# A new issue order for a hybrid attention and retention block, found with a longer price for short products

## The chip, the cores and the metric

The kernel runs on one core of one Trainium2 chip. The metric is the device time of one execution in microseconds (us); lower is better. Each time is a median over several executions. "TensorE" (PE in the profile) is the matmul engine, with its weight loads shown apart as PEld; "VectorE" is DVE, "ScalarE" ACT, "GpSimd" POOL; SP is the engine that issues most DMAs.

## The reference, cut to what matters

One decoder block over 512 tokens of 1024 channels, all float32, with one big input projection, two token mixers side by side, and a gated merge:

```python
h = rms_norm(x, norm_pre)
proj = h @ w_in                      # split into q, k, v, gates of both mixers
# mixer A, 8 heads of 64 in 2 groups
kc = compress_blocks(k_cmp_raw, ...) # 31 compressed keys and values per group
s  = einsum('qghd,cgd->qghc', qi, kc) * scale    # the short products of this change
p_c = masked_softmax(s, mask_c); o_c = einsum('qghc,cgd->qghd', p_c, vc)
# ... a selected and a sliding branch, each a masked softmax over up to 512 keys
o_a = g0 * o_c + g1 * o_s + g2 * o_w
# mixer B: retention, 4 heads of 128, chunks of 128 tokens
o_b = normalised(o_inner + o_cross)
y_a = (o_a * silu(z_n)) @ w_nsa_o ; y_b = (o_b * silu(z_r)) @ w_ret_o
merged = sigmoid(m_a) * y_a + sigmoid(m_b) * y_b
x = x + rms_norm(merged @ w_out, norm_post)
```

With 512 tokens there are 8 blocks of 64 keys and up to 16 may be selected, so every causal key is selected, so both long branches of mixer A are causal softmaxes over the same length.

## The kernel before

**Arithmetic.** Every float32 operand is split into a high and a low part (`whi`/`wlo`, `hTh`/`hTl`; ScalarE writes the high part, VectorE subtracts it to get the low part), and one product becomes three matmuls: high by high, high by low, low by high (`mm3`, line 313). Most matmuls have a 128 by 128 stationary operand and 512 moving columns.

**Stages on TensorE, in time.** The first projection `A` (keys and values, 512 columns), `C` (280 columns) and `Q`, the hidden layer of the compressed keys and values, then the weight blocks of `PLAN` (line 29): gate `Z`, `MA`, retention gate `ZR`, `QK`, `VR`, a seven-product block `PAIR` (line 1380), `VR` again, `MB`, and the output projections `NO`, `RO`, with two more seven-product blocks (`seven`), and last `out_seven` (line 1900). The seven-product blocks form sums of quarters of weight matrices with DRAM-to-DRAM accumulating DMAs that GpSimd issues (`add_sums`, lines 440 to 452).

**Work woven in between.** Attention runs between the projections' matmuls. For each tile of 128 queries, from the last to the first, `att_cmp` (line 1028) multiplies the queries of all eight heads with the compressed keys `kc`: seven products of 128 moving columns and one of 64, each with its own stationary operand. Retention does the like in `ret` (line 1406): per tile and head a product of 256 columns and one of 128 (lines 1442 and 1443). Transposes on TensorE (`tr`, line 310) go with nearly every step.

**What sets the order.** The order of all instructions of all engines is written out before launch by a planner, the class `Order` (line 63). Each piece of work is a coroutine that issues its instructions and yields the modelled time at which its next input is ready. `run` (line 135) takes the next coroutine by priority (`PRIOS`, or `OWN` for one instance, line 83) among those whose readiness plus a margin (`MARGINS`, or `OWN`) has passed on the planner's TensorE clock `now`. The main stream of projections has priority 9 and no margin, so it fills whatever is left. A margin is thus spare time between the modelled end of a producer and the place of its consumer in the order.

The planner's price of a matmul comes from `cols_ns` (line 300): where the last dimension of the moving operand is 2 (operands stored as two interleaved halves), 0.4167 ns a column and at least 112 ns; otherwise 0.4418 ns a column plus 2 ns. `mm` (line 305) uses it for more than 64 columns and takes 112 ns for 64 or fewer columns on a wide stationary operand. `PAIR` and `out_seven` use a fixed 215.8 ns.

Other constants that the change touches: `SOON`, `PSOON`, `CSOON` say how many weight halves ahead of the one wanted a split gets top priority (`rank`, line 601); `HOLD` is a pause in `tail_a` (line 835); `FIRST`, `HS`, `ASUMS` say at which point how many of the 27 weight sums are issued, and in which order (lines 435, 454, 1212): three after the signed halves of the input are written, then a group after gate `Z`, then some after each of the eight attention tiles, the rest during retention; `MORE` (line 474) says for which loads two additional weight tiles (named `shorts` in the profile) may be used; `EARLY_OUT` (line 1409) names the retention tiles whose values are first copied out of PSUM, scaled, to a spare buffer, so that the PSUM bank is free sooner.

Of the kernel before, what the change touches and what calls it, by code (L numbers as in the profile page):

```python
# [32 lines left out]
LAG, PE_LAG = 55.0, 60.0  # L33
TAIL = {"act": 110.0, "dve": 82.0, "pool": 45.0}
MARGIN = 20.0
MARGINS = {'att_cmp': 150.0, 'att_head': 150.0, 'att_out': 800.0, 'att_sum': 20.0, 'att_unit': 250.0, 'compress': 0.0, 'ga_split': 100.0, 'gates': 1300.0, 'h_sums': 1000.0, 'hidden': 400.0, 'keep': 600.0, 'kept': 1700.0, 'qk_end': 1300.0, 'ret': 50.0, 'ret_state': 50.0, 'rot_table': 250.0, 's_early': 400.0, 's_late': 1000.0, 'seven_end': 20.0, 'split_lo': 50.0, 'splitter': 250.0, 'tail_a': 50.0, 'tail_c': 0.0, 'tail_m': 1000.0, 'tail_o': 1700.0, 'tail_p': 1000.0, 'tail_q': 1000.0, 'tail_qk': 150.0, 'tail_yb': 600.0, 'tail_z': 100.0, 'x_split': 100.0, 'zr_end': 50.0}
SOON = 4
PSOON = 8
CSOON = 4
ISSUE = 8.0  # L40
SLACK = 1300
WAKE = 7
SIGN, SIGN_LAG = 3, 25000.0
HOLD_C = 300
EARLY = 300
HOLD = 1000
OSUMS = (0, 0, 0, 0, 0, 0, 1, 1)
W2_AT = 12
SUM_ON = 'dve'
ASUMS = (2, 2, 1, 1, 1, 1, 0, 0)  # L50
FIRST, BESIDE = 3, 3200.0
HS = (2, 7, 9)
DVE_BIAS = 700
PRIOS = {'att_block': 1, 'att_cmp': 3, 'att_head': 5, 'att_out': 1, 'att_sum': 1, 'att_unit': 0, 'attention': 2, 'compress': 1, 'edges': 0, 'flip': 5, 'ga_split': 5, 'gates': 5, 'h_low': 3, 'h_split': 5, 'h_sums': 2, 'hidden': 1, 'keep': 2, 'kept': 5, 'more_tiles': 5, 'norms': 2, 'qk_end': 1, 'ret': 2, 'ret_state': 0, 'rot_table': 0, 's_early': 1, 's_late': 2, 'seven_end': 1, 'tail_a': 0, 'tail_c': 1, 'tail_m': 2, 'tail_o': 0, 'tail_p': 3, 'tail_q': 0, 'tail_qk': 3, 'tail_ya': 5, 'tail_yb': 2, 'tail_z': 2, 'tail_zr': 0, 'weight_sums': 3, 'x_split': 2, 'zr_end': 5}
OWN = {'att_block.13': (1, None), 'att_block.21': (None, 20.0), 'att_block.33': (None, 600.0), 'att_block.34': (4, 0.0), 'att_block.36': (None, 150.0), 'att_block.37': (2, 0.0), 'att_block.38': (2, None), 'att_cmp.0': (5, None), 'att_cmp.1': (5, None), 'att_cmp.3': (2, 250.0), 'att_head.19': (1, None), 'att_head.44': (1, None), 'att_head.46': (None, 250.0), 'att_head.47': (None, 250.0), 'att_out.0': (None, 1000.0), 'att_sum.5': (None, 2200.0), 'att_sum.6': (0, 150.0), 'att_sum.7': (0, 600.0), 'att_unit.11': (5, 250.0), 'edges.0': (1, 20.0), 'ga_split.0': (1, 20.0), 'h_low.0': (0, 600.0), 'h_low.2': (2, 800.0), 'h_low.3': (1, 800.0), 'h_low.4': (None, 1000.0), 'h_split.0': (0, None), 'kept.0': (4, None), 'more_tiles.0': (None, 150.0), 'norms.0': (0, None), 'qk_end.0': (2, None), 'qk_end.1': (2, 1700.0), 'qk_end.2': (None, 20.0), 'qk_end.3': (2, None), 'ret.7': (5, 0.0), 'ret_state.2': (None, 150.0), 'ret_state.5': (None, 800.0), 'rot_table.2': (None, 0.0), 'rot_table.3': (0, None), 'rot_table.4': (0, 1700.0), 'signed.0': (4, 3000.0), 'signed.1': (0, 800.0), 'signed.2': (1, 250.0), 'signed.3': (None, 1000.0), 'signed.6': (None, 1300.0), 'split_lo.0': (4, 0.0), 'split_lo.1': (2, 1000.0), 'split_lo.100': (None, 0.0), 'split_lo.104': (None, 1300.0), 'split_lo.105': (2, 1300.0), 'split_lo.106': (None, 2200.0), 'split_lo.107': (3, 1300.0), 'split_lo.109': (None, 4500.0), 'split_lo.118': (0, 250.0), 'split_lo.121': (3, 400.0), 'split_lo.122': (4, None), 'split_lo.123': (0, 50.0), 'split_lo.124': (2, 150.0), 'split_lo.125': (None, 800.0), 'split_lo.127': (2, None), 'split_lo.128': (2, 800.0), 'split_lo.129': (None, 800.0), 'split_lo.130': (4, 150.0), 'split_lo.131': (2, None), 'split_lo.134': (None, 1700.0), 'split_lo.149': (None, 20.0), 'split_lo.160': (None, 100.0), 'split_lo.2': (0, 600.0), 'split_lo.203': (None, 400.0), 'split_lo.21': (None, 150.0), 'split_lo.22': (None, 800.0), 'split_lo.3': (None, 0.0), 'split_lo.4': (0, 100.0), 'split_lo.48': (None, 150.0), 'split_lo.52': (None, 50.0), 'split_lo.60': (None, 100.0), 'split_lo.68': (1, None), 'split_lo.69': (4, 20.0), 'split_lo.70': (2, 400.0), 'split_lo.74': (0, 0.0), 'split_lo.75': (None, 20.0), 'split_lo.76': (None, 800.0), 'split_lo.91': (0, None), 'split_lo.99': (None, 250.0), 'splitter.0': (1, 250.0), 'tail_a.3': (0, None), 'tail_c.2': (None, 100.0), 'tail_m.0': (None, 1000.0), 'tail_m.1': (1, None), 'tail_m.5': (0, 2200.0), 'tail_m.6': (5, 1000.0), 'tail_m.7': (2, 20.0), 'tail_q.0': (4, None), 'tail_q.1': (None, 800.0), 'tail_qk.0': (None, 250.0), 'tail_qk.2': (2, 20.0), 'tail_qk.3': (1, 150.0), 'tail_qk.4': (None, 2200.0), 'tail_qk.5': (3, 1000.0), 'tail_ya.0': (3, None), 'weight_sums.0': (2, 1700.0), 'x_split.0': (1, None), 'zr_end.0': (None, 150.0), 'zr_end.1': (4, 0.0), 'zr_end.3': (0, None)}
HFIRST, HWANT = 0, 0
MORE, MORE2 = range(12, 24), range(24, 28)
EARLY_OUT = ((0, 3), (1, 0), (1, 3))
SKEW = {'MA0': 4, 'Q': 4}
ROPES = ('dve', 'dve', 'dve')  # L60

# [1 line left out]
class Order:  # L63
# [16 lines left out]
    def spawn(self, gen, prio):  # L80
        k = gen.__name__
        i = self.seen[k] = self.seen.get(k, -1) + 1
        own = OWN.get(f"{k}.{i}", (None, None))
        first = PRIOS.get(k, prio) if own[0] is None else own[0]
        margin = MARGINS.get(k, MARGIN) if own[1] is None else own[1]
        self.cos.append([first, self.n, 0.0, gen, margin])
# [96 lines left out]
def block_kernel(ctx: ExitStack, tc, x, xT, x0s, ws, small, w2s, norm_post, rope_r, dmask, out):  # L183
# [47 lines left out]
    def size(a):  # L231
        n = 1
        for k in a.shape[1:]:
            n *= k
        return n
# [62 lines left out]
        return a.rearrange("p (a b) -> p a b", a=2)  # L298

    def cols_ns(b):  # L300
        return max(0.4167 * size(b) + 2.5, 112.0) if b.shape[-1] == 2 else 0.4418 * size(b) + 2

    def mm(ps, a, b, start, stop, r=0.0, cost=None):
        T.matmul(ps, a, b, start=start, stop=stop)  # L304
        return od.pe(cost or (cols_ns(b) if size(b) > 64 else 112 if a.shape[-1] > 64 else 54), r)
# [128 lines left out]
    seq = [(o, a, i >= 4) for s in (psums, sums, osums) for i, (o, a) in enumerate(s)]  # L434
    for i, h in zip(HS, hsums):
        seq[i:i] = [(*h, True)]
# [3 lines left out]
    def add_sums(n):  # L440

        for _ in range(n):
            o, a, add = seq[issued[0]]
            r = [landed.get(v.tensor.name, 0.0) for v in (o, a)]
            r = max(od.busy[v][1] + 1200 if isinstance(v, int) else v for v in r)
            if add:
                G.dma_start(o, a, accum_op=OP.add)
            else:
                G.dma_start(o, a)
            ns = (3200.0 if not add else 4600.0 if a.tensor.name.startswith("in_") else 5600.0) * size(o) / 2048  # L450
            landed[o.tensor.name] = od.sums(od.op("pool", 650.0, r), ns)
            issued[0] += 1

    def weight_sums():
# [7 lines left out]
        od.op("pool", 70.0, zready[0])  # L462
        add_sums(27 - FIRST - sum(OSUMS) - sum(ASUMS))
        od.flags.add("wsum")
# [136 lines left out]
    def rank(p):  # L601

        return lambda: 0 if p <= wanted[0] + (PSOON if p in pairp else CSOON if KD <= p < 2 * KD else SOON) else 4

# [195 lines left out]
    def keysT(kd, off, br, t, r):  # L800
        ps = yield from PT.get()
        yield r + PE_LAG
        for g in range(2):
            e = tr(ps[:, g * P:(g + 1) * P], kd[:, off + g * P:off + (g + 1) * P], ident, r)
        yield e, "act"
        v = ps[:, 0:256].rearrange("p (g c a) -> p g a c", g=2, a=2)
        sl = (slice(None), br, slice(None), slice(None), slice(t * 64, (t + 1) * 64))
        e = act(kA[sl], v, r=e)
        yield e, "dve"
        e = sub_split(kB[sl], v, kA[sl], e)  # L810
        PT.put(ps, e)
        return e
# [8 lines left out]
    def tail_a(t, ps, e, ring):  # L821
# [12 lines left out]
        NAT.put(kn, ev)  # L834
        yield e + HOLD
        yield from keysT(kd, 512, 0, t, e)
# [350 lines left out]
    def att_sum(t, g, po):  # L1187
# [16 lines left out]
        if all(n in od.flags for n in ATT):  # L1204
# [4 lines left out]
            for _ in range(2):  # L1209
                b = yield from PO.get()  # L1210
                PS.put(b)
        n = ASUMS[2 * (NT - 1 - t) + g]
        if n:
# [192 lines left out]
    def ret(hp, t, ps, e):  # L1406
        yield od.need(*[f"att{i}{g}" for i in (2, 3) for g in range(2)])
        vh, vl = yield from VR[hp].get()
        if (hp, t) in EARLY_OUT:
            vf = yield from NAT.get()  # L1410
# [761 lines left out]
```

## Time and profile before

| quantity | value |
|---|---|
| median of three runs | 480.07 us (478.75 to 480.45) |
| the profiled execution | 478.08 us |
| its span, first to last instruction | 476.3 us |
| TensorE busy | 468.8 us, 98% |
| VectorE busy | 411.1 us, 86% |
| ScalarE busy | 337.5 us, 71% |
| GpSimd busy | 43.9 us, 9% |
| mean granted TensorE clock | 0.997 |

The profiled execution took 1.8 us more than its span. Busy time of TensorE is a union of overlapping records: a matmul of 512 columns is recorded with 379 ns, while the next one starts 0.21 to 0.22 us after it. What a matmul costs the engine is therefore read from start to start.

### The profile page before, as it was taken

The page shows a single profiled execution, that of the slowest core. Times are in us where ns is not written, and L with a number is a line of the kernel's source. Part 1 is how long each engine was busy: PE and PEld are TensorE (multiplying, and loading weights), DVE is VectorE, ACT ScalarE, POOL GpSimd, SP SyncE. Part 2 cuts the span into 40 slices and gives each one's busy share as a digit, 9 for nine tenths or more (in the row PEclk, how much of TensorE's full clock was granted, in tenths as well). Part 3 has the DMA queues.
Part 4 walks back from the last instruction along what each step waited for, and adds up shares of the span by engine and source line. Part 5 has one row for each costly group of instructions (what it writes and reads, how often), then busy time and mean ns, then how long its engine had stood idle before and what let it go on. Part 6 is the DMA issues. An engine that isn't in the chain of part 4 may idle for free.

```text
span 476.3 us, 7891 instructions
## 1 busy us (share of the span) xinstructions
PE 468.8 (98%) x2686; PEld 420.1 (88%) x2686; DVE 411.1 (86%) x934; ACT 337.5 (71%) x724; POOL 43.9 (9%) x74
## 2 busy tenths in 40 slices
PE   9999999999999999999999999999999999999994
PEld 8899889988889888888989888998889999988884
DVE  6987899999798898898899998987687867989966
ACT  7976779887879899596698667755345536528853
POOL 3032004003020200101000000012000000000002
PEclk9999999999999999999999999999999999999998
DMA  8866865999997797544677671235974736605828
GB/s 304 330 232 200 261 237 178 290 280 286 322 307 152 143 325 240 111 140 129 135 259 251 203 221 56 67 111 98 326 284 138 230 119 205 202 37 178 253 102 176
DMA packets 30424, 96.65 MB, mean 203 GB/s; under 512 B 3088, under 2 KB 7056, under 8 KB 29584
## 3 DMA queue, kind: packets, MB, share of 16 engines
q1 hardware_dynamic: 23136, 66.66, 41.2%
q0 software_dynamic: 6960, 29.36, 25.8%
q8 instruction: 21, 0.34, 0.3%
q14 instruction: 19, 0.16, 0.1%
q10 hardware_dynamic: 288, 0.14, 0.1%
HBM read 91.42 MB, written 33.03 MB: 261 GB/s over the span
## 4 chain that ended last, share of the span: by engine, by line
PE 97%; DVE 1%; ACT 0%; issue 0%; DVEq 0%
PE bank L304 77%; PE bank L1380 8%; PE bank L1900 8%; PE bank L310 5%; PE bank L2040 1%; ACT whi L256 0%; DVE wlo L268 0%; DVE words L268 0%; DVE words L281 0%; ACT arena_r L256 0%; PE bank L2042 0%; DVE arena_r L268 0%; DVEq L2168 0%; DVE arena_r L264 0%; ACT rsrow L256 0%
## 5 line engine op out<-in xcount | busy, mean ns | idle before, releaser
L256 ACT ACTIVATE whi<-raw 128x512 fp32r<-128x512 f32 x176 | 106.8, 626 | 51.8 <-PE bank L304 34.4
L268 DVE TENSOR_TENSOR wlo<-raw,whi 128x512 fp32r<-128x512 f32 x182 | 119.2, 687 | 6.7 <-ACT whi L256 6.6
L304 PE MATMUL bank<-whi,hTh 128*128 128x512 f32 x192 | 72.1, 396 | 0.2 <-DVE words L268 0.2
L304 PE MATMUL bank<-whi,hTl 128*128 128x512 f32 x192 | 68.9, 379 | 0.0
L304 PE MATMUL bank<-wlo,hTh 128*128 128x512 f32 x192 | 68.8, 379 | 0.0
L304 PE MATMUL bank<-arena_r 128*128 128x256 f32 (+2 forms) x328 | 65.8, 323 | 0.2 <-DVE arena_r L268 0.2
L304 PE MATMUL bank<-arena_r,whi 128*128 128x512 f32 (+1 forms) x208 | 61.5, 371 | 0.0
L256 ACT ACTIVATE words<-words,stat 128x512 f32<-128x512 f32 (+3 forms) x107 | 55.9, 551 | 3.3 <-DVE stat L268 2.8
L256 ACT ACTIVATE arena_r<-bank 128x512 fp32r<-128x512 f32 (+3 forms) x87 | 45.6, 534 | 15.2 <-PE bank L310 14.8
L304 PEld LDWEIGHTS bank<-arena_r 128*128 128x128 f32 x328 | 50.3, 190 | 4.4 <-DVE arena_r L268 0.6
L268 DVE TENSOR_TENSOR arena_r<-bank,arena_r 128x512 fp32r<-128x512 f32 (+2 forms) x72 | 46.7, 656 | 8.7 <-ACT arena_r L256 8.2
L304 PEld LDWEIGHTS bank<-arena_r,whi 128*128 128x128 f32 x208 | 39.1, 189 | 5.0
L304 PE MATMUL bank<-hTh,whi 128*128 128x512 f32 (+1 forms) x120 | 41.5, 346 | 0.0
L304 PEld LDWEIGHTS bank<-whi,hTl 128*128 128x128 f32 x192 | 36.2, 189 | 5.1
L304 PEld LDWEIGHTS bank<-whi,hTh 128*128 128x128 f32 x192 | 36.5, 191 | 4.6 <-DVE words L268 0.8
L304 PE MATMUL bank<-hTl,whi 128*128 128x512 f32 (+1 forms) x120 | 40.5, 337 | 0.0
L304 PE MATMUL bank<-hTh,wlo 128*128 128x512 f32 (+1 forms) x120 | 40.5, 337 | 0.0
L304 PEld LDWEIGHTS bank<-wlo,hTh 128*128 128x128 f32 x192 | 36.4, 189 | 3.8
L268 DVE TENSOR_TENSOR words<-bank,words 128x512 f32<-128x512 f32 (+3 forms) x56 | 34.2, 616 | 6.0 <-ACT words L256 1.9
L268 DVE TENSOR_TENSOR words<-words,words 128x256 f32<-128x256 f32 (+5 forms) x73 | 35.9, 504 | 2.1 <-ACT rsrow L256 0.4
L310 PEld LDWEIGHTS bank<-identr,shorts 128*128 128x128 f32 x276 | 30.7, 140 | 6.6 <-DVE kc L281 0.3
L304 PE MATMUL bank<-arena_r,wlo 128*128 128x512 f32 x96 | 36.4, 379 | 0.0
(201 smaller groups left out, 926.7 us busy)
## 6 DMA issues: line engine op xcount, KB each, us to landing
raw<-in_stream_dram SPq DMA_DIRECT2D x73, 512.0 KB, 4.6
pair<-in_stream_dram POOLq DMA_DIRECT2D x6, 1024.0 KB, 9.5
t<-in_stream_dram POOLq DMA_DIRECT2D x6, 1024.0 KB, 17.7
out<-in_stream_dram POOLq DMA_DIRECT2D x6, 1024.0 KB, 11.3
raw<-s SPq DMA_DIRECT2D x8, 512.0 KB, 4.4
raw<-pair SPq DMA_DIRECT2D x8, 512.0 KB, 4.6
raw<-t SPq DMA_DIRECT2D x8, 512.0 KB, 4.5
raw<-out SPq DMA_DIRECT2D x8, 512.0 KB, 3.8
```

What stands on the lines that cost most here:

```text
L256: S.activation(o, i, func, **kw)
L268: (V if e == "dve" else G).tensor_tensor(o, a, b, op=op)
L304: T.matmul(ps, a, b, start=start, stop=stop)
L310: T.transpose(ps, a, idn)
L1380: T.matmul(ps[m], a, apart(b), start=n in first and s + j == 0, stop=n in last and s + j == 5, skip_group_check=True)
L1900: T.matmul(ps[m], a, apart(b), start=n in first and s + i == 0, stop=n in last and s + i == 5, skip_group_check=True)
L2040: T.matmul(banks[0][:, 0:P], rsrow[:, 0:P], rsrow[:, 0:P], start=True, stop=True)
```

## The change

One line of the planner's price list changes: a product whose moving operand isn't stored in interleaved halves now costs at least 106 ns. With 0.4418 ns a column plus 2, this touches products of 65 to 235 columns: the seven products of 128 columns per query tile with the compressed keys (28 in all), and the retention products of 128 columns (line 1443, 16 in all). Each was priced 58.5 ns and is now priced 106 ns. Then the constants that steer the order were chosen anew. No product is added, removed or changed in size. Of the constants, `MORE`, `EARLY_OUT`, `HS` and `ASUMS` change a little more than a place in the order: which buffer a weight half goes to, one copy out of PSUM, and where the weight sums are issued. The diff, with the long tables cut to the entries spoken of here:

```diff
-MARGINS = {
...
-'att_cmp': 150.0,
-'att_out': 800.0,
-'qk_end': 1300.0,
-'ret': 50.0,
-'splitter': 250.0,
-'tail_p': 1000.0,
-'tail_qk': 150.0,
...
+MARGINS = {
...
+'att_cmp': 400.0,
+'att_out': 150.0,
+'qk_end': 50.0,
+'ret': 20.0,
+'splitter': 1300.0,
+'tail_p': 150.0,
+'tail_qk': 400.0,
...
-SOON = 4
-PSOON = 8
-CSOON = 4
+SOON = 2
+PSOON = 5
+CSOON = 6
...
-HOLD = 1000
+HOLD = 800
...
-ASUMS = (2, 2, 1, 1, 1, 1, 0, 0)
+ASUMS = (6, 0, 2, 2, 2, 2, 0, 0)
 FIRST, BESIDE = 3, 3200.0
-HS = (2, 7, 9)
+HS = (0, 1, 2)
...
-PRIOS = {
...
-'h_split': 5,
-'norms': 2,
-'ret': 2,
...
+PRIOS = {
...
+'h_split': 0,
+'norms': 1,
+'ret': 5,
...
-MORE, MORE2 = range(12, 24), range(24, 28)
-EARLY_OUT = ((0, 3), (1, 0), (1, 3))
+MORE, MORE2 = range(12, 20), range(24, 28)
+EARLY_OUT = ((0, 3), (1, 3))
...
     def cols_ns(b):
-        return max(0.4167 * size(b) + 2.5, 112.0) if b.shape[-1] == 2 else 0.4418 * size(b) + 2
+        return max(0.4167 * size(b) + 2.5, 112.0) if b.shape[-1] == 2 else max(0.4418 * size(b) + 2, 106.0)
```

Of the 32 margins 23 change, of the 41 priorities 24, and of the table `OWN` of single instances 65 entries are changed, added or dropped.

More of the change, by code (lines that the diff above doesn't have):

```diff
@@ L35 @@
 MARGIN = 20.0
-MARGINS = {'att_cmp': 150.0, 'att_head': 150.0, 'att_out': 800.0, 'att_sum': 20.0, 'att_unit': 250.0, 'compress': 0.0, 'ga_split': 100.0, 'gates': 1300.0, 'h_sums': 1000.0, 'hidden': 400.0, 'keep': 600.0, 'kept': 1700.0, 'qk_end': 1300.0, 'ret': 50.0, 'ret_state': 50.0, 'rot_table': 250.0, 's_early': 400.0, 's_late': 1000.0, 'seven_end': 20.0, 'split_lo': 50.0, 'splitter': 250.0, 'tail_a': 50.0, 'tail_c': 0.0, 'tail_m': 1000.0, 'tail_o': 1700.0, 'tail_p': 1000.0, 'tail_q': 1000.0, 'tail_qk': 150.0, 'tail_yb': 600.0, 'tail_z': 100.0, 'x_split': 100.0, 'zr_end': 50.0}
-SOON = 4
-PSOON = 8
-CSOON = 4
+MARGINS = {'att_cmp': 400.0, 'att_head': 150.0, 'att_out': 150.0, 'att_sum': 0.0, 'att_unit': 250.0, 'compress': 20.0, 'ga_split': 20.0, 'gates': 1700.0, 'h_sums': 1300.0, 'hidden': 400.0, 'keep': 1300.0, 'kept': 1300.0, 'qk_end': 50.0, 'ret': 20.0, 'ret_state': 150.0, 'rot_table': 250.0, 's_early': 250.0, 's_late': 1300.0, 'seven_end': 600.0, 'split_lo': 50.0, 'splitter': 1300.0, 'tail_a': 50.0, 'tail_c': 0.0, 'tail_m': 1700.0, 'tail_o': 100.0, 'tail_p': 150.0, 'tail_q': 1000.0, 'tail_qk': 400.0, 'tail_yb': 250.0, 'tail_z': 400.0, 'x_split': 100.0, 'zr_end': 150.0}
+SOON = 2
+PSOON = 5
+CSOON = 6
 ISSUE = 8.0
@@ L49 @@
 SUM_ON = 'dve'
-ASUMS = (2, 2, 1, 1, 1, 1, 0, 0)
+ASUMS = (6, 0, 2, 2, 2, 2, 0, 0)
 FIRST, BESIDE = 3, 3200.0
-HS = (2, 7, 9)
+HS = (0, 1, 2)
 DVE_BIAS = 700
-PRIOS = {'att_block': 1, 'att_cmp': 3, 'att_head': 5, 'att_out': 1, 'att_sum': 1, 'att_unit': 0, 'attention': 2, 'compress': 1, 'edges': 0, 'flip': 5, 'ga_split': 5, 'gates': 5, 'h_low': 3, 'h_split': 5, 'h_sums': 2, 'hidden': 1, 'keep': 2, 'kept': 5, 'more_tiles': 5, 'norms': 2, 'qk_end': 1, 'ret': 2, 'ret_state': 0, 'rot_table': 0, 's_early': 1, 's_late': 2, 'seven_end': 1, 'tail_a': 0, 'tail_c': 1, 'tail_m': 2, 'tail_o': 0, 'tail_p': 3, 'tail_q': 0, 'tail_qk': 3, 'tail_ya': 5, 'tail_yb': 2, 'tail_z': 2, 'tail_zr': 0, 'weight_sums': 3, 'x_split': 2, 'zr_end': 5}
@@ new lines @@
+PRIOS = {'att_block': 1, 'att_cmp': 3, 'att_head': 5, 'att_out': 2, 'att_sum': 1, 'att_unit': 3, 'attention': 3, 'compress': 1, 'edges': 3, 'flip': 2, 'ga_split': 5, 'gates': 2, 'h_low': 1, 'h_split': 0, 'h_sums': 2, 'hidden': 0, 'keep': 0, 'kept': 3, 'more_tiles': 2, 'norms': 1, 'qk_end': 3, 'ret': 5, 'ret_state': 1, 'rot_table': 0, 's_early': 2, 's_late': 2, 'seven_end': 3, 'tail_a': 0, 'tail_c': 1, 'tail_m': 5, 'tail_o': 0, 'tail_p': 0, 'tail_q': 3, 'tail_qk': 3, 'tail_ya': 1, 'tail_yb': 5, 'tail_z': 2, 'tail_zr': 0, 'weight_sums': 2, 'x_split': 2, 'zr_end': 5}
@@ new lines @@
+OWN = {'att_block.13': (1, None), 'att_block.21': (None, 20.0), 'att_block.33': (None, 0.0), 'att_block.34': (4, 100.0), 'att_block.36': (None, 1000.0), 'att_block.37': (0, 0.0), 'att_block.38': (1, 400.0), 'att_block.39': (0, 20.0), 'att_cmp.0': (5, None), 'att_cmp.1': (5, None), 'att_cmp.3': (None, 0.0), 'att_head.19': (1, None), 'att_head.44': (1, None), 'att_head.45': (5, 50.0), 'att_head.47': (None, 1000.0), 'att_out.0': (3, 1300.0), 'att_sum.5': (None, 100.0), 'att_sum.6': (1, 2200.0), 'att_unit.11': (5, 600.0), 'edges.0': (4, 1700.0), 'ga_split.0': (1, 20.0), 'h_low.0': (5, 1700.0), 'h_low.1': (None, 20.0), 'h_low.2': (2, 800.0), 'h_low.3': (1, 800.0), 'h_low.4': (None, 1000.0), 'kept.0': (4, None), 'more_tiles.0': (3, 4500.0), 'norms.0': (1, 100.0), 'qk_end.0': (2, None), 'qk_end.1': (2, 1700.0), 'qk_end.2': (None, 20.0), 'qk_end.3': (3, None), 'ret.0': (2, 0.0), 'ret.7': (4, 100.0), 'ret_state.2': (None, 150.0), 'ret_state.5': (None, 800.0), 'rot_table.3': (1, 4500.0), 'rot_table.4': (0, 1700.0), 'signed.0': (0, 3000.0), 'signed.2': (1, 20.0), 'signed.3': (None, 1000.0), 'signed.6': (None, 1300.0), 'signed.7': (3, None), 'split_lo.0': (3, 150.0), 'split_lo.1': (0, None), 'split_lo.100': (None, 0.0), 'split_lo.104': (None, 1300.0), 'split_lo.105': (2, 1300.0), 'split_lo.106': (None, 2200.0), 'split_lo.107': (3, 1300.0), 'split_lo.109': (None, 4500.0), 'split_lo.110': (3, None), 'split_lo.111': (None, 1700.0), 'split_lo.116': (None, 600.0), 'split_lo.118': (0, 250.0), 'split_lo.121': (3, 400.0), 'split_lo.122': (4, None), 'split_lo.123': (0, 50.0), 'split_lo.124': (2, 150.0), 'split_lo.125': (None, 800.0), 'split_lo.126': (None, 1700.0), 'split_lo.127': (2, 1700.0), 'split_lo.128': (2, 1000.0), 'split_lo.129': (None, 20.0), 'split_lo.130': (4, 800.0), 'split_lo.131': (2, 1000.0), 'split_lo.134': (None, 1700.0), 'split_lo.149': (None, 20.0), 'split_lo.160': (None, 100.0), 'split_lo.162': (None, 50.0), 'split_lo.2': (0, 600.0), 'split_lo.203': (None, 400.0), 'split_lo.21': (None, 150.0), 'split_lo.22': (None, 800.0), 'split_lo.3': (None, 800.0), 'split_lo.4': (0, 100.0), 'split_lo.48': (None, 150.0), 'split_lo.52': (None, 50.0), 'split_lo.59': (None, 150.0), 'split_lo.60': (None, 100.0), 'split_lo.68': (1, None), 'split_lo.69': (4, 20.0), 'split_lo.70': (2, 400.0), 'split_lo.71': (None, 800.0), 'split_lo.73': (1, None), 'split_lo.75': (None, 1700.0), 'split_lo.76': (1, 400.0), 'split_lo.83': (None, 250.0), 'split_lo.91': (0, None), 'split_lo.99': (None, 250.0), 'splitter.0': (1, 400.0), 'tail_a.3': (0, None), 'tail_c.2': (None, 50.0), 'tail_m.1': (1, None), 'tail_m.5': (0, 2200.0), 'tail_m.7': (2, 20.0), 'tail_q.0': (4, None), 'tail_q.1': (3, 800.0), 'tail_qk.0': (None, 250.0), 'tail_qk.2': (0, 100.0), 'tail_qk.3': (1, 1000.0), 'tail_qk.4': (3, 2200.0), 'tail_qk.5': (3, 400.0), 'tail_qk.7': (0, None), 'tail_ya.0': (None, 100.0), 'x_split.0': (4, 0.0), 'zr_end.0': (None, 150.0), 'zr_end.1': (4, 0.0), 'zr_end.2': (None, 20.0), 'zr_end.3': (0, 1000.0)}
```

1 line of the change is left out of this document (removed).

## The prediction

> **What bounds the kernel now.** I read the page first: busy shares, the slices with the granted clock, the chain that ended last.
>
> ```profile
> span 476.3 us, 7891 instructions
> PE 468.8 (98%) x2686; PEld 420.1 (88%) x2686; DVE 411.1 (86%) x934; ACT 337.5 (71%) x724; POOL 43.9 (9%) x74
> PEclk9999999999999999999999999999999999999998
> PE 97%; DVE 1%; ACT 0%; issue 0%; DVEq 0%
> ```
>
> TensorE is busy almost from end to end, at full clock, and the chain runs 97% through it. Next I cut the span by stages (columns: stretch, length, then busy time of PE, PEld, DVE, ACT, POOL with counts, clock, DMA share, GB/s).
>
> ```profile
> 5.00:32.00 27.00, 27.00 (x148) 24.22 (x148) 25.35 (x58) 23.06 (x48) 3.55 (x5) 1.00 0.89 330
> 80.00:116.00 36.00, 36.00 (x223) 31.87 (x222) 34.01 (x83) 31.48 (x72) 4.95 (x6) 1.00 1.04 289
> 116.00:135.00 19.00, 18.76 (x105) 16.40 (x105) 15.62 (x42) 15.18 (x37) 5.50 (x7) 1.00 1.03 317
> 135.00:162.00 27.00, 27.00 (x162) 24.09 (x161) 24.19 (x70) 22.00 (x54) 2.05 (x4) 1.00 0.84 192
> 200.00:240.00 40.00, 39.82 (x228) 34.95 (x227) 35.38 (x77) 30.98 (x73) 2.42 (x3) 1.00 0.55 146
> 240.00:283.00 43.00, 43.00 (x229) 38.16 (x228) 41.40 (x80) 34.35 (x63) 2.09 (x3) 1.00 0.71 226
> 283.00:336.00 53.00, 53.00 (x300) 47.58 (x299) 45.41 (x99) 34.21 (x66) 5.47 (x8) 1.00 0.38 106
> 470.30:476.30 6.00, 0.00 (x0) 0.00 (x0) 2.73 (x6) 0.98 (x3) 0.00 (x0) 0.75 0.58 194
> ```
>
> Two stretches before the last alone show TensorE idle, 0.24 and 0.18 us. Since records overlap, I then looked at starts, in the order of time, around these two and at the beginning (start, duration, engine):
>
> ```profile
> 4.91 1.50 PE L304 MATMUL bank<-whi,hTh 128*128 128x512 f32 x4
> 6.25 1.03 PE L304 MATMUL bank<-whi,hTl 128*128 128x512 f32 x4
> ...
> 127.64 0.62 PE L310 MATMUL bank<-identr,shorts 128*128 128x128 f32 x6
> 128.10 0.45 PE L304 MATMUL bank<-hTh,whi 128*128 128x512 f32 x1
> 128.39 0.38 PE L304 MATMUL bank<-hTl,whi 128*128 128x512 f32 x1
> 128.60 0.38 PE L304 MATMUL bank<-hTh,wlo 128*128 128x512 f32 x1
> ...
> 130.12 0.38 PE L304 MATMUL bank<-arena_r 128*128 128x512 f32 x1
> 130.73 0.48 PE L304 MATMUL bank<-arena_r 128*128 128x512 f32 x1 [0.24 <-DVE arena_r L268]
> 131.05 0.38 PE L304 MATMUL bank<-arena_r,vcs 96*128 96x512 f32 x1
> ...
> 210.62 0.38 PE L304 MATMUL bank<-whi,hTl 128*128 128x512 f32 x1
> 211.17 0.48 PE L304 MATMUL bank<-whi,hTh 128*128 128x512 f32 x1 [0.18 <-DVE words L268]
> 211.49 0.38 PE L304 MATMUL bank<-wlo,hTh 128*128 128x512 f32 x1
> ```
>
> A product of 512 columns takes 0.21 us from start to start (128.39 to 128.60). So there are three real waits: 0.47 us at the head (4.91 to 6.25 is 1.34 for four products worth 0.87), 0.50 at 130.73 (0.61 and 0.32, each against 0.21), 0.44 at 211.17 (0.55 and 0.32). Together 1.4 us of 476. Besides, the first product after transposes starts its successor late: 128.10 to 128.39 is 0.29, so a change from transposes to products costs about 0.075 us.
>
> ```profile
> 31.84 0.12 PE bank L310 x2
> ...
> 335.92 0.30 PE bank L310 x4
> ```
>
> These are the first and last of the 74 pieces of transposes in the chain of waits: 74 x 0.075 = 5.5 us of changes. What is left is products back to back. [...]
>
> **The change part by part.**
>
> *TensorE's work: 0.* No product is added or removed, so an order can only win waits, changes to and from transposes, and the ends.
>
> *The new price of short products.* It acts through the plan alone. The rows for one query tile with the compressed keys, and for one retention tile:
>
> ```profile
> 111.53 0.97 PE L304 MATMUL bank<-kc,arena_r 128*128 128x128 f32 x8
> 112.34 0.46 PE L304 MATMUL bank<-hTh,whi 128*128 128x512 f32 x1
> ...
> 289.08 0.64 PE L304 MATMUL bank<-arena_r 128*128 128x256 f32 x4
> 289.56 0.43 PE L304 MATMUL bank<-whi,hTh 128*128 128x512 f32 x1
> ```
>
> The eight products take 0.81 us (111.53 to 112.34). The old plan gave them 7 x 58.5 + 112 = 0.52 us, the new one 7 x 106 + 112 = 0.85. So the old planner's clock ran ahead of the real engine by 0.29 us after each query tile, 4 x 0.29 = 1.2 us after the fourth; the new one is 0.04 a tile behind. This cuts both ways. A better clock lets the search see waits like the two above. But a planner that thinks TensorE earlier than it is leaves everything else up to 1.2 us of cover, and this cover is gone. For retention the four products take 0.48 us; the old plan had 2 x (115.1 + 58.5) = 0.35, the new one 0.44; again the new price is nearer, and 8 tiles x 0.09 = 0.8 us of cover goes.
>
> [...]
>
> *The two waits in the middle, 0.94 us, and new ones.* No row of before shows the new waits. Bounds: all 0.94 us go and none comes (-0.94), or the lost cover shows as waits, +1.2 on top. I take -0.4: the first wait stands in the attention whose clock is now right, and is the nearer row. The head's 0.47 stays: its operands come from the first transfers.
>
> *Transposes.* Their count is fixed; how many pieces they fall into is not. Five pieces more or fewer is 5 x 0.075 = 0.4 us. I take 0.
>
> *Weight sums (`ASUMS`, `HS`).* Six sums move from behind gate Z (80 us) to the first finished attention tile (about 135 us), and the three sums of the input come first. Loads beside sums land late:
>
> ```profile
> raw<-in_stream_dram SPq DMA_DIRECT2D x10, 512.0 KB, 11.3
> ...
> raw<-in_stream_dram SPq DMA_DIRECT2D x10, 512.0 KB, 4.4
> ```
>
> 11.3 us is the median at 80 to 116 us, 4.4 at 240 to 280. Yet TensorE was busy 36.00 of 36.00 us there, with the DMA share at 1.04. So the loads run far enough ahead to hide 7 us. On GpSimd's queue the sums stand ahead of small retention operations (from 229 us), but the groups of two end before. Value 0; if a load beside six sums came another 7 us later than its cover, that is the bound, +7, which I hold unlikely because the share at 135 to 162 us was 0.84 where 80 to 116 stood 1.04.
>
> *`MORE`.* The two additional tiles are withheld from the second hidden weights (loads 20 to 23). Before, no hidden product used them: both groups, 32 + 32, read `whi`/`wlo`.
>
> ```profile
> L304 PE MATMUL bank<-whi,arena_r 128*128 128x256 f32 x32 | 7.8, 279 | 0.0
> L304 PE MATMUL bank<-wlo,arena_r 128*128 128x256 f32 x32 | 7.7, 275 | 0.0
> ```
>
> So 0. *`EARLY_OUT`.* One copy out of PSUM falls away at retention tile (1, 0): at most one ScalarE operation of about 0.6 us, in a stretch where ScalarE works 34.21 of 53 us; the bank is held one VectorE operation (0.69) longer. 0, bounds -0.1 and +0.7.
>
> *The end.* From the last product to the end 6.0 us pass, in which only norms, the final scaling and the stores are left, in an order set by their inputs: 0 +-0.3.
>
> The sum: -0.4, so span 475.9 and 477.7 for an execution like the profiled one (478.08). That execution is 2.0 us under the median of the three, 480.07; I put the same -0.4 on the median: **479.7**.
>
> **The rivals.**
>
> *No effect at all* (the new order is as good as the old by chance, waits as before): 480.1. For it: 1.4 us of waits are all that an order could have cured.
>
> *Faster.* The search also joins transposes. All 0.94 us of waits go, and 25 pieces of 74 vanish: 25 x 0.075 = 1.9. 480.07 - 2.8 = 477.2. For it: most pieces have four transposes, some eight, so joining is possible. Against: a joined piece needs two blocks ready and two banks free at once. [...]
>
> *Slower: weight halves split too late.* `SOON` goes from 4 to 2 and `PSOON` from 8 to 5, and the splitter's margin from 250 to 1300 ns. A half gets top priority only two (in `PAIR` five) halves ahead. A half lasts TensorE 6 x 0.216 = 1.3 us, so in the plain blocks 2.6 us of cover are left where 5.2 were, and a split takes a ScalarE and a VectorE operation one after the other:
>
> ```profile
> L256 ACT ACTIVATE whi<-raw 128x512 fp32r<-128x512 f32 x176 | 106.8, 626 | 51.8 <-PE bank L304 34.4
> L268 DVE TENSOR_TENSOR wlo<-raw,whi 128x512 fp32r<-128x512 f32 x182 | 119.2, 687 | 6.7 <-ACT whi L256 6.6
> ```
>
> That is 1.3 us if neither queue is backed up. The place is 80 to 116 and 240 to 283 us, where VectorE is busy 34.01 of 36 and 41.40 of 43. It decides from the point where VectorE's queue ahead of a split exceeds the other 1.3 us, two operations. Each half then late by one operation stops TensorE 0.69 us. Six such halves of 182: +4.1, with the -0.4: 483.8. From four on (+2.4) it is slower by over 0.5%. Against: lower priority delays only where something else is ready.
>
> *Slightly slower at the head.* `h_split` and `norms` change priority where DMA share is 0.89; one ScalarE and VectorE operation out of place costs 1.3 us: 481.0.
>
> **How the numbers follow.** About 0.5% (2.4 us, below 477.7 or above 482.5) is what a measurement of this kernel can tell from no change. Chances: forecast 479.7, 0.47; no effect 480.1, 0.14; faster 477.2, 0.18; late splits 483.8, 0.13; head 481.0, 0.08. The three single runs before spread over 1.7 us, so the middle cases leak a little over either bound, 0.02 down and 0.05 up. Faster 0.20, same 0.62, slower 0.18. The range takes in the faster case and half of the slower one: 477.0 to 483.2; the forecast's own is 478.7 to 481.3 (-0.94 - 0.4 to +1.2).
>
> **What would show it.** Right: TensorE busy 98% again, 2686 products, the wait near 130 us gone or moved, VectorE's and ScalarE's busy time within 1 us, pieces of transposes in the chain between 69 and 79. Forecast wrong: three or more waits `PE <- DVE wlo` (late splits); under 50 pieces (joined transposes); TensorE waiting on raw loads or on `hTh` in the first 32 us; raw loads at 135 to 180 us landing over 11.3 us with TensorE idle beside them (sums). If the 512-column spacing itself changed from 0.21 us, the whole argument would fall.

## The result, and the profile after

| | before | after |
|---|---|---|
| median of 18 executions each | 479.24 us (477.79 to 480.45) | 481.38 us (479.78 to 485.05) |
| ratio, 95% interval | | 1.0051 (1.0037 to 1.0065) |
| the profiled execution | 478.08 us | 485.05 us |
| its span | 476.3 us | 483.3 us |

The changed kernel is slower by 0.5%, about 2.1 us. The profiled execution of the changed kernel is the slowest of its 18, so what it shows has to be weighed against the median: 2.1 us are to be explained, not 7.

The page of the changed kernel, the lines that answer to those of before (busy shares, granted clock in 40 slices, chain that ended last by engine):

```profile
PE 472.7 (98%) x2686; PEld 422.6 (87%) x2686; DVE 413.1 (85%) x938; ACT 333.7 (69%) x719; POOL 43.8 (9%) x73
PEclk8999999999999999999899999999999999999999
PE 95%; DMA 3%; DVE 1%; issue 0%; SPq 0%; ACT 0%; DVEq 0%; ACTq 0%
```

The work is the same 2686 products. But the chain holds DMA for 3%, where before had none, and the clock has two slices below 9, the first one and one in the middle. Cut by stages (stretch, length, busy time and count of PE, PEld, DVE, ACT, POOL, clock, DMA share, GB/s):

```profile
0.00:20.00 20.00, 17.64 (x73) 14.94 (x74) 15.64 (x30) 15.91 (x30) 4.21 (x17) 0.91 0.92 343
20.00:216.00 196.00, 196.00 (x1157) 175.01 (x1156) 177.25 (x496) 157.07 (x389) 27.21 (x40) 1.00 0.78 222
216.00:229.00 13.00, 12.39 (x65) 10.49 (x64) 10.57 (x19) 6.78 (x17) 0.00 (x0) 1.00 1.03 281
229.00:231.40 2.40, 0.81 (x8) 0.56 (x6) 0.45 (x2) 0.47 (x2) 0.00 (x0) 1.00 0.15 51
231.40:236.40 5.00, 5.00 (x20) 4.32 (x21) 4.09 (x11) 3.93 (x9) 0.73 (x1) 0.66 0.00 0
```

From 20 to 216 us TensorE is never idle, all of attention and the waits at 130 us included. What is lost lies in the first 20 us, at 216 to 229, and above all at 229.00 to 231.40, where TensorE is busy for 0.81 of 2.40 us, and in the 5 us behind it, at a clock of 0.66. The waits of TensorE, then the chain around that place (start, duration, what):

```profile
PE bank L304 <- ACT arena_r L256: 1.6, 1, 1.6
PE bank L304 <- DVE hTl L281: 1.2, 1, 1.2
...
PE bank L304 <- DVE arena_r L281: 0.6, 1, 0.6
```

```profile
219.80 10.52 DMA words<-in_dmask_dram
...
230.41 0.44 DVE words L268
...
230.93 0.42 ACT arena_r L256
...
231.40 8.51 PE bank L304 x37
```

The first retention tile waits for the decay mask (`dm`, line 1205): one load of 256 KB that takes 10.5 us. In before the same load took 3.4 us. What else was on the way, in the transfers issued from 195 to 235 us (KB each, median us to landing), first before, then after:

```profile
out<-in_stream_dram POOLq DMA_DIRECT2D x2, 1024.0 KB, 8.4
...
raw<-s SPq DMA_DIRECT2D x1, 512.0 KB, 4.7
words<-in_dmask_dram SPq DMA_DIRECT2D x1, 256.0 KB, 3.4
```

```profile
out<-in_stream_dram POOLq DMA_DIRECT2D x4, 1024.0 KB, 9.7
...
raw<-s SPq DMA_DIRECT2D x1, 512.0 KB, 12.6
raw<-pair SPq DMA_DIRECT2D x1, 512.0 KB, 11.5
words<-in_dmask_dram SPq DMA_DIRECT2D x1, 256.0 KB, 10.5
```

After has two transfers of the sums more in this stretch. Two of the four, sums 23 and 24, are issued together at 209.00 us, behind the sixth attention tile (the sixth entry of `ASUMS` is now 2 where it was 1). Before issues its own two at 194.5 and 223.8 us, so no sum begins beside its mask, which is loaded from 218.7 to 222.1. On SyncE's queue the mask follows `raw<-s` (issued at 215.66) and `raw<-pair` (218.11), and all three land one behind the other (228.3, 229.6 and 230.3 us).

At the head the wait of 0.47 us has become larger in this execution:

```profile
1.62 4.04 DMA raw<-in_stream_dram
...
5.69 0.44 DVE whi L264
...
6.76 0.49 DVE hTl L281
...
7.29 4.74 PE bank L304 x13
```

VectorE now makes both parts of the second weight half (the high `whi` and the low `wlo`) before the low part `hTl` of the input, where before only `whi` stood ahead of it, and the second piece of the stream landed at 5.66 us. TensorE stands until 7.29.

### The profile page after: what moved, and what is told of

It reads as the page before. It is cut to its first block, busy times and chain, and to the rows that moved or that the text cites. A ratio compares the mean times of both kernels' runs of the same rounds, so it can differ in the third digit from the quotient of the medians.

```text
span 483.3 us, 7888 instructions
## 1 busy us (share of the span) xinstructions
PE 472.7 (98%) x2686; PEld 422.6 (87%) x2686; DVE 413.1 (85%) x938; ACT 333.7 (69%) x719; POOL 43.8 (9%) x73
## 4 chain that ended last, share of the span: by engine, by line
PE 95%; DMA 3%; DVE 1%; issue 0%; SPq 0%; ACT 0%; DVEq 0%; ACTq 0%
PE bank L304 75%; PE bank L1380 8%; PE bank L1900 8%; PE bank L310 5%; DMA words<-in_dmask_dram 2%; DMA raw<-in_stream_dram 1%; DVE words L281 0%; DVE words L268 0%; DVEq L2168 0%; DVE hTl L281 0%; DVE whi L264 0%; ACT arena_r L256 0%; SPq L673 0%; SPq L503 0%; ACT rsrow L256 0%
## 5 line engine op out<-in xcount | busy, mean ns | idle before, releaser
L256 ACT ACTIVATE whi<-raw 128x512 fp32r<-128x512 f32 x172 | 103.8, 625 | 56.8 <-PE bank L304 40.1
L304 PE MATMUL bank<-whi,hTl 128*128 128x512 f32 x192 | 70.4, 388 | 1.2 <-DVE hTl L281 1.2
L304 PE MATMUL bank<-wlo,hTh 128*128 128x512 f32 x192 | 70.1, 386 | 0.0
L304 PE MATMUL bank<-arena_r 128*128 128x512 f32 (+2 forms) x328 | 66.7, 327 | 1.6 <-ACT arena_r L256 1.6
L256 ACT ACTIVATE words<-words,stat 128x128 f32<-128x128 f32 (+3 forms) x107 | 55.0, 546 | 5.9 <-DVE stat L1103 2.9
```

What stands on the lines that cost most here:

```text
L256: S.activation(o, i, func, **kw)
```

## The experiments

Each was timed in turn with the kernel before on the same chip. The theories of the first four: **A**, the loss sits at the two places shown, the mask's load and the head; **B**, the profiled execution shows an accident, and the loss is spread over late weight splits. Of the later ones: **C**, a load without cover beside sums; its rivals stand in each expectation.

### The changed kernel again, the two sums later, the head, and both

The first run is the changed kernel, unedited. The second holds back sums 23 and 24 and issues them behind the first retention tile; all engines but GpSimd keep their order.

```diff
+LATER = (23, 24)
 ... in add_sums
+            if issued[0] in LATER: held.append((o, a))
-            if add:
+            elif add:
 ... in ret, behind the statistics of a tile
+        [G.dma_start(*held.pop(0), accum_op=OP.add) for _ in held[:]]
         add_sums(OSUMS[4 * hp + t])
```

The third moves one VectorE operation (`wlo` of the second weight half) behind the two `hTl`; the fourth does both.

```diff
-            r = sub_split(vl, src, vh, r)
+            r = sub_split(vl, src, vh, r) if p != 1 else (lo1.append((vl, src, f(vh))), ...)[1]
 ... where hTl of a part is done
+        [V.tensor_tensor(*lo1.pop(), op=OP.subtract) for _ in lo1[:] if k == 0]
         od.flags.add(f"h{k}")
```

> The changed kernel as it is, once more. Theory A (two places: the mask load of retention lands late beside two weight sums, and at the head one VectorE operation stands ahead of the low part of the input): the profile again shows TensorE waiting over 1 us near 231 us, with the mask load landing in some 10 us, and 1.0 to 1.4 us near 7 us; time about 2.1 us over before. Rival B (the two waits are an accident of the one slow execution profiled; the usual loss is spread over late weight splits): neither wait in this profile, several waits on wlo instead, time about 2.1 us over before all the same.

> The changed kernel with only the two last weight sums before retention issued later: behind the first retention tile's small GpSimd operation (about 234 us) in place of 209 us; all other engines keep their order. A: the mask load lands in 3 to 4 us, the wait near 231 us is gone, 1.8 us less in an execution of full clock, up to 4 less where the clock had dropped; median 1.5 to 2 us under the changed kernel. B: no change of the median (within 0.4 us).

> The changed kernel with only one VectorE operation moved: the low part of the second weight half goes behind the two operations that make the low part of the first input block, as in the kernel before. A: the wait at the head shrinks by that operation, 0.7 us; median 0.6 to 0.9 us under the changed kernel, more where the clock had dropped at the head. B: no change (within 0.4 us).

> Both moves together. A: the gains add, 2.2 to 2.8 us under the changed kernel, so within 0.5 us of before or a little under. B: no change, 2.1 us over before.

| run | median us | ratio to before, 95% |
|---|---|---|
| changed kernel again | 482.31 | 1.0065 (1.0039 to 1.0091) |
| sums later | 483.87 | 1.0103 (1.0077 to 1.0128) |
| head | 481.19 | 1.0046 (1.0024 to 1.0069) |
| both | 483.33 | 1.0082 (1.0058 to 1.0106) |

In the changed kernel's second profile no wait for `hTl` is listed at the head and the clock has 9 in the first slice (the first 137 products take 26.43 us, from 5.15 to 31.58, where the profiled execution needs 26.62 for 133 of them, from 7.29 to 33.91), but the wait for the mask is there again. Its load and the products (start, duration) that meet it:

```profile
217.35 10.80 DMA words<-in_dmask_dram
```

```profile
226.90 0.46 PE L310 MATMUL bank<-identr,shorts 128*128 128x128 f32 x4
229.23 1.84 PE L304 MATMUL bank<-arena_r 128*128 128x256 f32 x12 [1.88 <-ACT arena_r L256]
```

So the mask isn't an accident of one execution. The long wait at the head is one that comes and goes (1.20 us in the profiled execution, 1.4 in that of the run with the sums later, none here), and the run with the head changed can't be told from the unchanged one (intervals overlap). The run with the sums moved was meant to be faster and was slower. Its mask wait is gone, but the sums now stand beside another load, issued only when the split before it has freed its buffer (its chain of waits, then its stages):

```profile
236.35 8.90 DMA raw<-pair
...
246.48 0.58 ACT words L256
...
247.11 4.98 PE bank L1380 x14
```

```profile
244.20:247.11 2.91, 0.23 (x3) 0.01 (x1) 1.12 (x2) 1.75 (x4) 0.00 (x0) 1.00 1.03 305
247.11:251.50 4.39, 4.39 (x13) 3.57 (x14) 2.61 (x5) 3.35 (x6) 0.00 (x0) 0.61 0.85 332
```

TensorE stands for nearly 2.7 us and then works 4.4 us at a clock of 0.61. The place of the sums matters, then, but the first other place that was tried was no better.

### Both sums in a stretch with room, and their mirror in the kernel before

The first holds the same two sums until the first two retention tiles of the second pair (297.5 and 309.4 us), one behind each. Only GpSimd's order differs from the changed kernel. The lines show what differs from the run with the sums later.

```diff
-        [G.dma_start(*held.pop(0), accum_op=OP.add) for _ in held[:]]
+        [G.dma_start(*held.pop(0), accum_op=OP.add) for _ in held[:1] if hp]
```

The second is the kernel before, with its own two sums 23 and 24 (at 194 and 224 us) issued together at 208 us.

```diff
+            if issued[0] in LATER: pass
 ... in rot_table
+        if i == 2: G.tensor_copy(mark, rtab[:, 0:1]), [G.dma_start(*seq[j][:2], accum_op=OP.add) for j in LATER]
```

> The changed kernel with the two sums moved further: one behind each of the first two retention tiles of the second pair of heads (about 303 and 315 us), nothing else moved. Theory C (the mask load and then the loads of the summed weights have no cover; two sums of 1 MB at once in front of them cost a wait, and there is a place for them where nothing is short): mask load in 3 to 4 us, no wait near 231 us and none near 247 us; 1.5 to 2.3 us under the changed kernel, ratio to before about 1.001 to 1.003. Rival D (the new order has no room: wherever the two sums go, some load is late): a wait of 2 us or more at another place, ratio 1.005 or more.

> The mirror: the kernel before with its two sums of this kind (194 and 224 us) issued together at about 208 us, 10 us ahead of its mask load; PE, VectorE, ScalarE and SP keep their order. C: the mask load lands in about 10 us in place of 3.4, TensorE waits 1.5 to 3.5 us near 230 us; ratio 1.004 to 1.008. D, or any theory in which the collision matters only in the new order: no change, within 0.15%.

The first measured 479.16 us beside 479.30, ratio 1.0000 (0.9988 to 1.0013). All of the loss is gone, with every other edit of the change still in. Its transfers in the same stretch, and the stages around it:

```profile
raw<-s SPq DMA_DIRECT2D x1, 512.0 KB, 4.4
raw<-pair SPq DMA_DIRECT2D x1, 512.0 KB, 4.4
words<-in_dmask_dram SPq DMA_DIRECT2D x1, 256.0 KB, 3.4
```

```profile
216.00:224.00 8.00, 7.39 (x41) 6.17 (x40) 6.79 (x11) 4.15 (x9) 0.00 (x0) 1.00 0.40 137
224.00:236.00 12.00, 12.00 (x70) 10.72 (x69) 8.83 (x22) 8.40 (x18) 0.73 (x1) 1.00 0.08 22
```

The mirror cost 487.72 us, ratio 1.0180 (1.0160 to 1.0201), 8.4 us more than before. It was expected to be slower, but the load that paid was another one than expected: in this order the rope table, not the mask, is issued as the sums begin.

```profile
211.22 12.04 DMA words<-in_rope_r_dram
```

```profile
words<-in_rope_r_dram SPq DMA_DIRECT2D x3, 256.0 KB, 2.7
...
words<-in_dmask_dram SPq DMA_DIRECT2D x1, 256.0 KB, 3.0
```

```profile
224.61 1.63 PE L304 MATMUL bank<-arena_r 128*128 128x512 f32 x2 [6.15 <-ACT arena_r L256]
```

The median of the three tables issued from 195 to 235 us is 2.7 us, the one beside the sums took 12.04, and TensorE waited 6.15 us for it; the mask, issued later, took 3.0. In both orders two sums beside a load without cover went with lost time; how much (2.1 and 8.4 us), and on which load, differs.

### The price alone, and the constants alone

The kernel before with the new price and all its old constants, and the changed kernel with the old price and all its new constants (the one line of `cols_ns`, as the diff of the change has it, forwards and backwards).

> The kernel before with the new price alone, all other constants as before, so that the planner writes a new order with the old sums. C: the price by itself is harmless, mask load in 3 to 5 us, ratio 0.998 to 1.002. Rival E (the longer price took the 1.2 us of cover that the short one gave): small waits of 0.3 to 0.6 us behind the compressed attention, ratio 1.002 to 1.005.

> The changed kernel's constants with the old price. C: the sums stand where they stood, so the mask load is late again and TensorE waits 1 to 2.5 us near 230 us; ratio 1.003 to 1.008. E: the cover is back and the ratio falls to 1.002 or less.

The price alone: 486.91 us, ratio 1.0148 (1.0110 to 1.0186). The constants alone: 484.45 us, 1.0110 (1.0090 to 1.0131). Both ratios lie outside what was expected. Two of TensorE's waits with the price alone, and the chain of waits behind the longest one:

```profile
PE bank L304 <- DVE arena_r L268: 2.5, 2, 1.7
PE bank L304 <- DVE arena_r L281: 1.6, 1, 1.6
```

```profile
101.67 13.70 DMA raw<-in_stream_dram
...
118.99 0.48 PE bank L304
```

Its mask load took 3.6 us, so this loss is another one: VectorE results of attention that come late. The longest of these waits goes back to a load after all. A raw load took 13.7 us (the kernel before has sums under way from 105 us on), and four weight splits on VectorE (2.50 us from 115.83) then went ahead of the attention result that TensorE needed at 118.99.

With the constants alone, theory C was right about the mask: it took 8.2 us, landed at 227.4, and TensorE waited 1.1 us for it at 228.45. What C left out are two more waits for VectorE, 1.6 us at 214.25 and 1.1 at 222.76. The new price isn't better or worse by itself in these two runs, and either half of the change without the other makes several waits of 1 to 2 us; that margins and priorities fit only the price they were chosen with is the likely reason, not a tested one.

### One sum instead of two

The changed kernel, with sum 23 at its place and only 24 moved to the second pair (`LATER = (24,)`).

> The changed kernel with one of the two sums behind the sixth attention tile left there and the other one moved to the first retention tile of the second pair. A dose. Theory C (the load of the mask has no cover, and what it loses to sums beside it is lost on TensorE): with one sum beside it the mask load takes between the 3.4 us without and the 10 us with two, about 5.5 to 7 us; its wait of TensorE is then the load's excess less the cover. With two sums, 9.6 to 10.8 us of load gave waits of 0.8 to 2.0 us, so the cover ends near 8.8 us; 5.5 to 7 us of load gives no wait, and the time is that of the kernel with both sums moved, ratio 1.000 (0.998 to 1.002). Rival (each sum at this place costs by itself, half of the loss): the ratio lies between, 1.003, with a wait of about 0.5 to 1 us near 231 us.

479.22 us, ratio 1.0008 (0.9989 to 1.0027).

```profile
words<-in_dmask_dram SPq DMA_DIRECT2D x1, 256.0 KB, 5.7
```

In the executions profiled of kernels that keep the changed kernel's order up to here, the mask takes 3.4 us with no sum beside it, 5.7 with one and 9.6 to 10.8 with two. The time of these runs follows the load's cover and not the number of sums: with one sum nothing is lost.

### The mask early, the sums where they are

The changed kernel with the mask loaded into another buffer behind the fourth attention tile. The sums stay at 209 us, and the order on TensorE, VectorE, ScalarE and GpSimd stays. Attention's later tiles write into that buffer too, so the retention scores are multiplied with other values than the mask; the operations, their sizes and places are the same.

```diff
-    dm = at(20, 512).rearrange("p (h c) -> p h c", h=4)
+    dm = at(18, 512).rearrange("p (h c) -> p h c", h=4)
 ... in att_sum
-        od.flags.add(f"att{t}{g}")
+        od.flags.add(f"att{t}{g}"), (t, g) == (2, 1) and DMA.dma_start(dm, ...)
         if all(n in od.flags for n in ATT):
-            DMA.dma_start(dm, dmask.rearrange("h p c -> p h c"))
```

> The changed kernel with all its sums where they are, and the mask of the retention scores loaded into another buffer, which is free from the first norms on, behind the fourth attention tile instead of the last one (on SyncE's queue it then stands five raw loads earlier; the order on TensorE, VectorE, ScalarE and GpSimd stays). Theory C (the loss is the mask's load without cover beside the two sums): the mask is there long before retention, no wait at 229 to 231 us although both sums still run from 209 us, raw loads beside them still take 12 us without TensorE waiting, and the time is 479.2 with a kernel before of 479.2, ratio 1.000 (0.998 to 1.002). Rival H (the two sums cost by themselves, by whatever comes next: another load without cover, a rope table or a raw half, takes the place of the mask): a wait of 1 us or more in 225 to 250 us on another load and a ratio of 1.003 to 1.006.

479.04 us, ratio 1.0006 (0.9992 to 1.0020). The transfers from 195 to 235 us, and the products at the place of the wait:

```profile
out<-in_stream_dram POOLq DMA_DIRECT2D x2, 1024.0 KB, 15.4
...
raw<-s SPq DMA_DIRECT2D x1, 512.0 KB, 12.9
raw<-pair SPq DMA_DIRECT2D x1, 512.0 KB, 11.5
```

```profile
227.02 0.46 PE L310 MATMUL bank<-identr,shorts 128*128 128x128 f32 x4
227.32 1.57 PE L304 MATMUL bank<-arena_r 128*128 128x256 f32 x12
228.72 0.38 PE L304 MATMUL bank<-whi,hTh 128*128 128x512 f32 x1
```

The sums are there, the raw loads beside them take 12.9 and 11.5 us as in the changed kernel, and nothing waits: from transposes to retention 0.30 us pass, where the changed kernel's second profile has 2.33. This run names the one load. It also gives the mask's cover: retention can start at 227.32, the two short operations between took 1.08 us (230.32 to 231.40 in the changed kernel), and the mask was asked for at 217.4 in the runs with this beginning; so it has some 8.8 us. 3.4 and 5.7 fit, 9.6 to 10.8 don't.

### The two waits that remain

In the run with both sums moved, one wait is left in the middle, 0.86 us by starts, at 219.94: a product of the main stream waits for a PSUM bank that retention tile (0, 0) holds through a VectorE operation (line 281). First the values were copied out by ScalarE to a spare buffer, so that the bank is free sooner; then, on top, both parts of the second weight half were moved behind `hTl` at the head.

```diff
-            e = act(vh, ps, r=e, scale=rs(t))
+            e = act(vh if hp + t else at(18, 512), ps, r=e, scale=rs(t)), hp + t or S.activation(vh, at(18, 512), AF.Copy)
 ... VectorE's subtraction for this tile then reads at(18, 512) in place of ps
```

> The changed kernel with both sums moved to the retention tiles of the second pair, and the values of retention tile (0, 0) first copied out of PSUM to a spare buffer, so that the bank is free after one ScalarE operation (one ScalarE operation more; nothing else differs). Theory F (the wait of 0.86 us near 220 us for a PSUM bank that one VectorE operation holds is a loss by itself): the wait shrinks to about 0.1 us, 0.7 us less than with the sums moved alone, 478.4 us for a kernel before of 479.2, ratio 0.9985. Rival G (TensorE then meets the next late thing): a wait of 0.5 us or more appears within the next 10 us and the ratio stays 1.000.

> The run before this one, with the high and low part of the second weight half moved on VectorE behind the two low parts of the hidden input (only VectorE's order in the first 10 us differs). Theory A (the head's wait, 1.20 us in the profiled execution of the changed kernel, comes when the second piece of the stream lands late and VectorE waits for it ahead of hTl): the first products wait for hTl no longer than before (start 4.9 to 6.3 us, 0.47 us lost), and the mean goes down by 0.2 to 1.0 us, to about 478.0, ratio 0.997. Rival (the piece lands in time in most executions, and the products of the second half now wait instead): no difference from the run before, within 0.3 us.

They measured 479.12 us, 1.0002 (0.9984 to 1.0020), and 479.19 us, 0.9999 (0.9981 to 1.0016), beside 479.22 of the one-sum run on the same chip: nothing gained. The stretch at 216 to 224 us is full now, and the next one isn't (both changes in):

```profile
216.00:224.00 8.00, 8.00 (x43) 6.77 (x42) 6.09 (x11) 4.73 (x9) 0.00 (x0) 1.00 0.35 120
224.00:232.00 8.00, 7.76 (x45) 6.53 (x44) 6.48 (x17) 4.92 (x11) 0.72 (x1) 1.00 0.11 33
```

```profile
226.12 0.46 PE L310 MATMUL bank<-identr,shorts 128*128 128x128 f32 x4
226.81 1.84 PE L304 MATMUL bank<-arena_r 128*128 128x256 f32 x12 [0.24 <-ACT arena_r L256]
228.49 0.38 PE L304 MATMUL bank<-whi,hTh 128*128 128x512 f32 x1
```

TensorE arrives at the first retention tile 0.9 us sooner than with the mask early (226.12 against 227.02) and finds its masked scores not ready: 0.69 us from transposes to retention instead of 0.30, and twelve products in 1.68 us instead of 1.40. The wait was moved, not removed. At the head the rival's "no difference" fits, and again the loss was moved: the first four products lose only 0.31 us (4.64 to 5.82), but a later group of four loses 0.51 (7.55 to 8.93), where TensorE waits for the next `hTl`.

## Why the prediction was wrong

The forecast was a gain of 0.4 us, and measured was a loss of 2.1. The measured 481.38 lies within the stated 477.0 to 483.2, but by luck: this range was drawn to take in half of the late weight splits, and the rival nearest in number, the head at 481.0, isn't what moves the median. The base was off too: 480.07 was the median of three executions, and that of 18 is 479.24.

**The step that failed is the weight sums, "Value 0".** It priced one kind of load, the raw weights, and reasoned that they "run far enough ahead to hide 7 us". For them that holds: in the changed kernel `raw<-s` took 12.6 us and, with the mask early, 12.9, and TensorE didn't wait. (In the order that the price alone gives it fails even for a raw load, the one of 13.7 us.) It doesn't hold for a load that can't be asked for early, and the sum had no term for these. The mask is one: its buffer belongs to attention until the last tile, so it is issued at 219.80 and used 11.6 us later, with 8.8 us of cover. The rope table (12.04 us) and the later `raw<-pair` (8.90) are others, as the mirror and the moved sums show. The place was missed as well: the text looked for late loads beside the six sums behind the first tile (135 to 180 us, all 45 us busy). The groups of two, one of them behind the sixth tile, it weighed on GpSimd's queue alone, and not for the loads beside them. The bound of +7 was there, but as "a load beside six sums".

The size then follows by steps. The changed kernel's second profile (481.20 us, span 479.4, the lowest of its six times) and the run with both sums moved (478.98, span 477.2) differ by 2.2 us, and the mask's wait by starts is 2.0 of it (2.33 less the 0.30). In the slowest execution 1.75 us of wait (2.05 less 0.30) brought another 2.0 at the slow clock (from the first retention product to the seventh 512-column product behind it 4.65 us, with the mask early 2.70), and the head 2.4 more (the fourth group of four products starts at 10.79, with the sums moved at 8.38): 6.1 of the 6.1 us between the spans 483.3 and 477.2.

**TensorE's work: right.** 2686 products; those of 512 columns are 0.21 to 0.22 us apart in the rows read at a full granted clock (128.51 to 128.94 in the changed kernel, 230.91 to 233.50 in its second profile).

**The waits in the middle, -0.4: right in sign at one place, wrong in sum.** The wait at 130.73 is gone: 116 to 135 us is busy throughout, where before lacked 0.24. But the one at 211.17 (0.44) has its like in the wait for a bank, 0.86, so the sum is nearly 0, and the run with both sums moved, which is the new order without its flaw, is as fast as before (1.0000, 0.9988 to 1.0013). The range of this term holds; the gain didn't come.

**The new price: right that it cuts both ways, far too small.** "Up to 1.2 us of cover" was worked out as if the constants stood still. With the constants still, the price alone costs 7.6 us (486.91 to 479.30), through VectorE results of attention that come late, which is the kind of loss named, at six times its size. A planner's clock is not an additive cost: the new price writes another order for everything behind it. That it is the nearer of the two prices stays: the eight products with the compressed keys take 0.88 us in the changed kernel (112.31 to 113.19), 110 ns on average, beside the 106 and 58.5 of the two plans.

**The head, "stays": wrong.** VectorE's new order puts `wlo` of the second weight half, too, ahead of `hTl`, behind the wait for a transfer. Counted by starts as the 0.47 us of before was, the loss is 2.01 us in the profiled execution (4.41 to 7.29 less 0.87) and 0.83 in that of the run with both sums moved (4.91 to 6.61). What it does to the median the experiments can't tell from nothing.

**Transposes, `MORE`, the end: right.** 71 pieces of transposes in the chain where 74 were; the last product to the end takes 6.0 us with the sums moved, as before. `EARLY_OUT`: no wait at retention tile (1, 0); the bank that is waited for is that of tile (0, 0), which the change left alone. The sign that VectorE's and ScalarE's busy time stay within 1 us failed (411.1 to 413.1 and 337.5 to 333.7), but with the sums moved they are 413.0 and 333.2 and the time is that of before, so this isn't the loss.

**The rivals.** Late weight splits: no profile of the changed kernel has a wait on `wlo`, so the smaller `SOON`, `PSOON` and the larger margin did no harm that shows. No effect: right, in sum, for all of the change except two DMAs. Slower at the head: a place that does lose, yet not what moves the median, since with the sums moved and the head as it is the loss is gone. None of the rivals was the mask, and "raw loads landing over 11.3 us with TensorE idle" named the right sign, long loads beside sums, for the wrong load.

## What to carry to other kernels

When a change moves bulk transfers, list every load that will be under way beside them, and for each the time from when it can first be issued to when it is needed; here one load of 256 KB whose buffer comes free late, with 8.8 us of cover and 10.5 us to landing, set the price of the move. A constant that was chosen by search seems to belong to the model it was searched with: the price alone cost 1.5% here and the constants alone 1.1%, together they cost 0.5%, and all of that was one pair of DMAs. A wait removed just ahead of another dependency was paid there: of the 0.86 us gone at 219.94, 0.67 came back at the masked scores (0.69 for 0.30 and 1.68 for 1.40).

## What the runs showed of the hardware

**A short stand of TensorE cost more than its length in four places, and not in two others.** After 1.59 us idle in the profiled execution, 2.68 in the run with the sums moved by one tile, and 6.15 in the mirror, products of 512 columns were 0.43 us apart for 3 to 5 us, where their spacing is otherwise 0.21 to 0.22. The granted clock in these stretches is 0.66, 0.61 and 0.57:

```profile
224.61:230.00 5.39, 5.34 (x16) 3.85 (x17) 4.81 (x9) 2.76 (x6) 0.00 (x0) 0.57 0.62 208
```

At the head of the profiled execution it was 1.20 us idle: from 7.29 to 10.79 the clock is 0.51. Yet after the 1.88 us of the changed kernel's second profile the products of 512 columns are 0.21 to 0.22 us apart (230.91 to 233.50), with a clock of 1.00 from 229.2 to 240. After 1.4 us at the head of the run with the sums moved by one tile the clock has 9 in the first slice, and 133 products take 24.95 us (7.76 to 32.71), where the profiled execution needs 26.62 for them. So length alone doesn't decide; what does, no run here shows.

**Three loads beside two sums took 7 to 8 us longer.** With two sums of 1 MB under way, `raw<-s`, `raw<-pair` and the mask, issued within 4.2 us on SyncE's queue, landed at 228.3, 229.6 and 230.3 us, in this order. They took 12.6, 11.5 and 10.5 us; in the run with both sums moved, issued as close together, they took 4.4, 4.4 and 3.4. How much of the mask's 10.5 us is the sums and how much the two raw loads ahead of it wasn't measured apart; the nearest row is the 5.7 us with one sum.
